# Where 16 weight slots lie in SBUF, modulo 256 bytes

## The chip, the cores and the metric

The kernel runs on one core of a Trainium2 chip. Its time is in device microseconds, from the first to the last instruction with the little around them; runs are compared by their medians. A core has TensorE (PE in the profile, with weight loads apart as PEld), VectorE (DVE), ScalarE (ACT), GpSimd (POOL) and SyncE (SP, which issues the DMAs here). SBUF is the on-chip memory: 128 partitions, and in each a range of byte addresses. A tile takes the same byte range in every partition.

## What is computed

A decoder trunk of 4 layers on 256 tokens of width 1024, in float32. Each layer has three sublayers: a half-step SwiGLU FFN, a token mixer (latent attention, differential attention, Mamba-2, latent attention), and another half-step FFN. So 12 sublayers stand in a row, and each needs the one before it.

```python
cond = silu(c)
for i in range(4):
    mod = (cond @ w_mod[i] + b_mod[i]).reshape(-1, 3, 3, 1024)   # shift, scale, gate
    for j, f in enumerate((ffn(i, 0), mixer(i), ffn(i, 1))):
        h = x * (1 + scale_j) + shift_j
        x = layernorm(8 ** 0.25 * x + weight_j * gate_j * f(h), ln_g[i, j], ln_b[i, j])

def ffn(h):                                  # w_in (1024, 5632), w_out (2816, 1024)
    gate, up = split(h @ w_in)
    return (silu(gate) * up) @ w_out
```

All weights are read once from HBM, about 500 MB in float32 together with `w_mod`.

## The kernel before

**Precision and the three matmuls.** Every product with a weight matrix is made of two fp32r parts of each operand, a high and a low one. For each block of 128x128 weights `mm3` issues three matmuls into one PSUM bank: high weights with high rows, high weights with low rows, low weights with high rows. The weights are the stationary operand. The rows that stream past them are 256 tokens wide (258 in the first products of a sublayer, which carry two more columns).

**Tiles.** `Slots` makes a row of tiles of one kind in SBUF, one behind the other, and hands them out. `wraw` (8 slots of 4096 bytes a partition) receives raw weights from DMA. `wr` (16 slots of 4096 bytes) holds the split weights: ScalarE writes the high part into one slot, VectorE the low part into another. A half-item is one `wraw` slot, thus two `wr` slots, which are nearly always a pair, slots 2p and 2p+1. `hwh` and `hwl` hold the high and low part of the rows that enter a sublayer; `g` has 25 slots that hold, among other things, the high and low rows for the second product of an FFN or a mixer. In most of the kernel a half-item has four 128-row blocks of two 128-column blocks, so 4 x 2 x 3 = 24 matmuls.

**Addresses.** Tiles stand in SBUF in the order in which they are made: `g`, `wraw`, `gacc`, `res`, `t256`, `sd`, `re`, `hwh`, `hwl`, then `wr`, then small tiles and constants. Every tile ahead of `wr` is a multiple of 256 bytes long, so they all begin at the same place modulo 256, and so does the first `wr` slot. `WSTEP = 16` (L422) puts 16 float32, 64 bytes, behind every second slot:

```python
for i in range(n):
    self.tiles.append(self.make(i, dt))
    if step and i % 2:
        pool.tile([128, step], F32, name=f"{name}gap{i}", tag=f"{name}gap{i}")
```

Counted from the streaming rows modulo 256, the eight pairs thus begin at 0, 64, 128, 192, 0, 64, 128, 192. Within a slot a 128x128 block begins at a multiple of 512 bytes, and so does a 256-column row in `hwh`, `hwl` and `g`. Rows of the 258-column products lie 1152 bytes apart.

**Order.** `Program` records all operations, gives each a slot (the one that has been free longest) and an engine, and plans their times with a table of costs; then it issues them in the order of the planned starts. Neither slots nor costs know an address. All instructions stand on the line of that loop, L400.

**Background.** Between the weights, `w_mod` streams through `wraw`, and VectorE sums it up into `gacc` for the shifts, scales and gates of later sublayers.

Of the kernel before, what the change touches and what calls it, by code (L numbers as in the profile page):

```python
# [10 lines left out]
F32 = mybir.dt.float32  # L11
F32R = mybir.dt.float32r
# [43 lines left out]
class Ref:  # L56


    def __init__(self, root, fns):
        self.root, self.fns, self.ap = root, fns, None  # L60
# [52 lines left out]
class Slots:  # L113

    def __init__(self, pool, name, n, elems, psum=False, dt=F32, fresh=False, step=0):
        self.pool, self.name, self.elems, self.psum, self.dt, self.fresh = pool, name, elems, psum, dt, fresh
        self.tiles = []
        for i in range(n):  # L120
            self.tiles.append(self.make(i, dt))
            if step and i % 2:
                pool.tile([128, step], F32, name=f"{name}gap{i}", tag=f"{name}gap{i}")
        self.free = list(range(n))
        self.hist, self.old, self.owner = [[] for _ in range(n)], [[] for _ in range(n)], [None] * n

# [292 lines left out]

WHOLE = (4, 7, 10)  # L420

WSTEP = 16  # L422

DEFER = {0: 3, 1: 3}

# [2 lines left out]
def trunk(ctx: ExitStack, tc: tile.TileContext, consts, x, c, positions, w_mod, b_mod, ln_g, ln_b,  # L428
# [8 lines left out]
    sb = ctx.enter_context(tc.tile_pool(name="sb", bufs=1))  # L437
    pp = ctx.enter_context(tc.tile_pool(name="pp", bufs=1, space=PSUM))
    PW, HP = S + 2, 288
    slots = {}  # L440

    def pool(name, n, elems, dt=F32, step=0):
        slots[name] = Slots(sb, name, n, elems, dt=dt, fresh=name == "g", step=step)

    slots["mm"] = slots["aux"] = Slots(pp, "mm", 8, 512, True)
    for name, n, elems in (("g", 25, 512), ("wraw", 8, 1024), ("gacc", 1, 3072), ("res", 1, 2048),
                           ("t256", 14, 256), ("sd", 1, 512), ("re", 1, 512)):
        pool(name, n, elems)
    for name, n, elems in (("hwh", 1, KD * HP), ("hwl", 1, KD * HP)):
        pool(name, n, elems, F32R)  # L450
    pool("wr", 16, 1024, F32R, WSTEP)
    for name, n, elems in (("dtr", 1, 128), ("w0", 1, 32), ("modc", 6, 24)):
        pool(name, n, elems)

# [308 lines left out]
    class Tail:  # L763
        def __init__(self, s, res, weight):
            self.s, self.d = s, res
            self.weight, self.w = weight, None
# [878 lines left out]
```

## Time and profile before

| | |
|---|---|
| median of 3 runs | 2103.96 us (2102.66 to 2103.96) |
| the profiled execution's own time | 2103.96 us |
| its span, first to last instruction | 2102.2 us |
| TensorE busy | 2074.9 us, 99% |
| VectorE busy | 1713.0 us, 81% |
| ScalarE busy | 1190.2 us, 57% |
| DMA, mean over the span | 240 GB/s |
[...]

How to read it: matmuls are pipelined. [...] How fast the matmuls go through is seen from the distance of their starts (timeline) or from their number in a stretch (table by stretch). The timeline merges neighbours of one kind into one row; in the FFN's first product `hwl` comes once among three matmuls, so it has rows of its own.

### The profile page before, as it was taken

How to read it: one execution, taken by the hardware profiler on the slowest of the kernel's cores; microseconds unless marked ns; L12 is line 12 of the kernel's file. 1: busy time of each engine (PE TensorE's matmuls, PEld its weight loads, DVE VectorE, ACT ScalarE, POOL GpSimd, SP SyncE). 2: the span in 40 equal slices, each digit the busy share in tenths (PEclk: the TensorE clock that was granted, in tenths of full speed). 3: DMA queues.
4: the chain of work that ended last, by engine and by line, in shares of the span. 5: the costliest groups of instructions: out<-in, count | busy, mean ns of one | idle time of the engine just before them, and what ended most of it. 6: DMA issues, size and time to landing. Idle time of an engine off the chain costs nothing. (4 is left out here: it accounts for less than half of the span.)

```text
span 2102.2 us, 42927 instructions
## 1 busy us (share of the span) xinstructions
PE 2074.9 (99%) x17287; PEld 2011.6 (96%) x17287; DVE 1713.0 (81%) x2745; ACT 1190.2 (57%) x1836; POOL 98.5 (5%) x112
## 2 busy tenths in 40 slices
PE   8999999999999999999999999999999999999998
PEld 6999999999999999999999988899999999999998
DVE  4888899887887879977988798879887988879744
ACT  3554687536544786644654475547545644577543
POOL 0000100000000101000000011000000000100000
PEclk9999999999999999999999999999999999999999
DMA  9899657995989435997698654356986889545861
GB/s 312 281 346 326 206 188 249 342 304 187 319 309 324 149 103 161 350 326 256 191 354 304 206 159 140 112 157 197 355 281 205 302 305 323 163 130 186 261 186 45
DMA packets 410227, 504.58 MB, mean 240 GB/s; under 512 B 21937, under 2 KB 371244, under 8 KB 410028
## 3 DMA queue, kind: packets, MB, share of 16 engines
q1 hardware_dynamic: 410028, 501.84, 72.5%
q8 instruction: 135, 2.21, 0.4%
q14 instruction: 64, 0.52, 0.1%
HBM read 500.73 MB, written 1.05 MB: 239 GB/s over the span
## 5 line engine op out<-in xcount | busy, mean ns | idle before, releaser
L400 PE MATMUL mm<-hwh,wr 128*128 128x256 f32 (+1 forms) x6736 | 1222.2, 283 | 3.7 <-ACT hwh L400 1.9
L400 PEld LDWEIGHTS mm<-hwh,wr 128*128 128x128 f32 x6736 | 1041.1, 189 | 19.9 <-issue 14.1
L400 ACT ACTIVATE wr<-wraw 128x1024 fp32r<-128x1024 f32 (+3 forms) x705 | 700.7, 1003 | 577.2 <-PE mm L400 242.9
L400 PE MATMUL mm<-hwl,wr 128*128 128x256 f32 (+1 forms) x3368 | 955.7, 284 | 4.9 <-DVE hwl L400 4.8
L400 DVE TENSOR_TENSOR wr<-wraw,wr 128x1024 fp32r<-128x1024 f32 (+3 forms) x691 | 793.7, 1165 | 172.4 <-ACT wr L400 169.1
L400 PE MATMUL mm<-g,wr 128*128 128x256 f32 x5496 | 665.2, 282 | 1.4 <-DVE g L400 0.9
L400 PEld LDWEIGHTS mm<-g,wr 128*128 128x128 f32 x5496 | 652.9, 189 | 12.3 <-issue 8.3
L400 PEld LDWEIGHTS mm<-hwl,wr 128*128 128x128 f32 x3368 | 637.4, 189 | 11.1 <-DVE hwl L400 6.8
L400 DVE SCALAR_TENSOR_TENSOR gacc<-wraw,condc,gacc 128x1024 f32<-128x1024 f32 x238 | 307.2, 1291 | 7.9 <-DMA wraw<-in_w_mod_dram 7.2
L400 ACT ACTIVATE g<-mm 128x512 f32<-128x512 f32 (+4 forms) x208 | 105.7, 521 | 100.3 <-PE mm L400 98.7
L400 ACT ACTIVATE g<-g 128x512 fp32r<-128x512 f32 (+1 forms) x104 | 63.3, 625 | 36.0 <-DVE g L400 35.6
L400 PE MATMUL mm<-g,g 128*128 128x128 f32 (+2 forms) x464 | 81.6, 312 | 0.0
L400 DVE TENSOR_TENSOR g<-g,g 128x512 fp32r<-128x512 f32 (+2 forms) x111 | 75.4, 699 | 4.2 <-ACT g L400 3.4
L400 DVE TENSOR_TENSOR res<-res,re 128x256 f32<-128x256 f32 x171 | 68.0, 418 | 8.2 <-ACT re L400 7.9
L400 DVE TENSOR_TENSOR g<-g,mm 128x512 f32<-128x512 f32 x81 | 54.9, 680 | 19.6 <-PE mm L400 16.9
L400 PEld LDWEIGHTS mm<-g,g 128*128 128x128 f32 (+1 forms) x464 | 57.9, 175 | 7.4 <-ACT g L400 0.5
L400 ACT ACTIVATE t<-res 128x256 f32<-128x256 f32 x84 | 34.8, 416 | 48.1 <-DVE res L400 47.9
L400 POOL TENSOR_TENSOR res<-res,t 128x256 f32<-128x256 f32 x28 | 25.4, 932 | 708.9 <-ACT t L400 624.9
L400 DVE TENSOR_TENSOR res<-res,t 128x256 f32<-128x256 f32 x56 | 31.7, 581 | 23.9 <-ACT t L400 23.9
L400 DVE SCALAR_TENSOR_TENSOR res<-mm,gw,res 128x256 f32<-128x256 f32 x84 | 39.2, 475 | 14.2 <-PE mm L400 14.2
L400 ACT ACTIVATE t<-res,abcol 128x256 f32<-128x256 f32 x72 | 43.2, 601 | 9.3 <-DVE res L400 8.0
L400 ACT ACTIVATE res<-res,abcol 128x256 f32<-128x256 f32 x88 | 48.0, 588 | 0.0
(198 smaller groups left out, 1158.5 us busy)
## 6 DMA issues: line engine op xcount, KB each, us to landing
wraw<-in_ffn_w_in_dram SPq DMA_DIRECT2D x340, 512.0 KB, 6.1
wraw<-in_w_mod_dram SPq DMA_DIRECT2D x272, 512.0 KB, 6.8
wraw<-in_ffn_w_out_dram SPq DMA_DIRECT2D x128, 512.0 KB, 5.7
wraw<-in_ffn_w_out_dram SPq DMA_DIRECT2D x64, 384.0 KB, 5.7
wraw<-in_ssm_w_in_dram SPq DMA_DIRECT2D x32, 512.0 KB, 4.3
wraw<-in_diff_w_in_dram SPq DMA_DIRECT2D x24, 512.0 KB, 4.3
wraw<-in_w_mod_dram SPq DMA_DIRECT2D x32, 256.0 KB, 6.2
wraw<-in_mla_w_out_dram SPq DMA_DIRECT2D x16, 512.0 KB, 4.6
```

Source lines behind the costliest of these rows:

```text
L400: getattr(eng.real, method)(*[real(a) for a in args], **{k: real(v) for k, v in one.items()})
```

## The change

The gap behind every second slot becomes a list of gaps ahead of slots, `WGAPS`. The first pair has 16 float32 (64 bytes) ahead of it, each later pair 32 (128 bytes). Counted from the streaming rows modulo 256, the pairs now begin at 64, 192, 64, 192, 64, 192, 64, 192. All gaps together grow from 512 to 960 bytes, so everything that is made after `wr` (constants and small tiles) moves up by 448 bytes.

```diff
-    def __init__(self, pool, name, n, elems, psum=False, dt=F32, fresh=False, step=0):
+    def __init__(self, pool, name, n, elems, psum=False, dt=F32, fresh=False, gaps=()):
         self.tiles = []
         for i in range(n):
+            if gaps and gaps[i]:
+                pool.tile([128, gaps[i]], F32, name=f"{name}gap{i}", tag=f"{name}gap{i}")
             self.tiles.append(self.make(i, dt))
-            if step and i % 2:
-                pool.tile([128, step], F32, name=f"{name}gap{i}", tag=f"{name}gap{i}")
...
-WSTEP = 16
+WGAPS = [16, 0] + [32, 0] * 7
...
-    pool("wr", 16, 1024, F32R, WSTEP)
+    pool("wr", 16, 1024, F32R, WGAPS)
```

The instructions do not move. TensorE, before the change, in the first product of an FFN, where it goes over from pair 7 (`wr14`, `wr15`) to pair 1 (`wr2`, `wr3`); `mm` are PSUM banks, and the last number of a name counts the tiles in the order in which they were made:

```order
L400 MATMUL mm1_62<-hwh0_120,wr15_144 128x256
L400 MATMUL mm1_62<-hwh0_120,wr14_143 128x256
L400 MATMUL mm1_62<-hwl0_121,wr14_143 128x256
L400 MATMUL mm1_62<-hwh0_120,wr15_144 128x256
L400 MATMUL mm7_68<-hwh0_120,wr2_125 128x256
L400 MATMUL mm7_68<-hwl0_121,wr2_125 128x256
L400 MATMUL mm7_68<-hwh0_120,wr3_126 128x256
```

The same place of TensorE's order after the change:

```order
L400 MATMUL mm1_62<-hwh0_120,wr15_145 128x256
L400 MATMUL mm1_62<-hwh0_120,wr14_144 128x256
L400 MATMUL mm1_62<-hwl0_121,wr14_144 128x256
L400 MATMUL mm1_62<-hwh0_120,wr15_145 128x256
L400 MATMUL mm7_68<-hwh0_120,wr2_126 128x256
L400 MATMUL mm7_68<-hwl0_121,wr2_126 128x256
L400 MATMUL mm7_68<-hwh0_120,wr3_127 128x256
```

Slots, banks and order are the same; only the count in the slots' names is one higher, since a gap now stands ahead of the first slot. The other four engines' orders are equal in the same sense.

## Rows read from the trace of the kernel before

**Rows 1.** The page: span and busy shares of the engines.

```profile
span 2102.2 us, 42927 instructions
PE 2074.9 (99%) x17287; PEld 2011.6 (96%) x17287; DVE 1713.0 (81%) x2745; ACT 1190.2 (57%) x1836; POOL 98.5 (5%) x112
```

**Rows 2.** Groups by shape: xcount | busy us, mean ns | idle before, releasers.

```profile
L400 PE MATMUL mm<-hwh,wr 128*128 128x256 f32 x5984 | 1082.5, 283 | 3.7 <-ACT hwh L400 1.9 <-ACT g L400 1.0 <-DVE wr L400 0.5
...
L400 PE MATMUL mm<-hwl,wr 128*128 128x256 f32 x2992 | 847.3, 283 | 1.8 <-DVE hwl L400 1.8
...
L400 PE MATMUL mm<-g,wr 128*128 128x256 f32 x5496 | 665.2, 282 | 1.4 <-DVE g L400 0.9 <-ACT g L400 0.2
...
L400 PE MATMUL mm<-hwh,wr 128*128 128x258 f32 x752 | 141.0, 285 | 0.0
```

**Rows 3.** By stretch: us, PE, PEld, DVE, ACT, POOL busy, clock, DMA share, GB/s.

```profile
850.00:1000.00 150.00, 150.00 (x1269) 148.44 (x1268) 121.26 (x142) 72.86 (x90) 1.86 (x2) 1.00 0.90 308
1050.00:1200.00 150.00, 150.00 (x1293) 147.84 (x1292) 124.36 (x158) 75.96 (x98) 5.53 (x5) 1.00 0.90 302
1450.00:1600.00 150.00, 150.00 (x1274) 148.49 (x1273) 122.21 (x134) 73.06 (x88) 0.00 (x0) 1.00 0.94 321
```

**Rows 4.** Timeline of TensorE, FFN at 1453 us: start us, length us, operation.

```profile
1453.79 0.28 PE L400 MATMUL mm<-hwl,wr 128*128 128x256 f32 x1
...
1456.62 0.28 PE L400 MATMUL mm<-hwl,wr 128*128 128x256 f32 x1
...
1459.45 0.28 PE L400 MATMUL mm<-hwl,wr 128*128 128x256 f32 x1
...
1462.32 0.27 PE L400 MATMUL mm<-hwl,wr 128*128 128x256 f32 x1
...
1465.16 0.28 PE L400 MATMUL mm<-hwl,wr 128*128 128x256 f32 x1
...
1467.98 0.28 PE L400 MATMUL mm<-hwl,wr 128*128 128x256 f32 x1
...
1470.36 0.28 PE L400 MATMUL mm<-hwl,wr 128*128 128x256 f32 x1
```

**Rows 5.** Timeline of TensorE, FFN at 358 us, pair 7 then pair 1.

```profile
358.62 0.28 PE L400 MATMUL mm<-hwl,wr 128*128 128x256 f32 x1
...
361.34 0.28 PE L400 MATMUL mm<-hwl,wr 128*128 128x256 f32 x1
...
363.72 0.28 PE L400 MATMUL mm<-hwl,wr 128*128 128x256 f32 x1
```

**Rows 6.** Timeline of TensorE, Mamba-2 mixer at 1256 us, pair 7 then pair 1.

```profile
1256.35 0.44 PE L400 MATMUL mm<-g,g 128*64 128x128 f32 x4
...
1257.30 0.28 PE L400 MATMUL mm<-hwl,wr 128*128 128x256 f32 x1
...
1258.72 0.28 PE L400 MATMUL mm<-hwl,wr 128*128 128x256 f32 x1
...
1261.19 0.28 PE L400 MATMUL mm<-hwl,wr 128*128 128x256 f32 x1
```

**Rows 7.** By stretch of 50 us, columns as in rows 3.

```profile
300.00:350.00 50.00, 48.40 (x408) 47.19 (x407) 48.09 (x99) 37.35 (x64) 3.30 (x4) 1.00 0.67 212
350.00:400.00 50.00, 50.00 (x430) 50.00 (x430) 47.52 (x51) 29.68 (x35) 1.33 (x1) 1.00 1.02 359
...
1100.00:1150.00 50.00, 50.00 (x435) 48.85 (x434) 44.29 (x52) 22.11 (x26) 0.56 (x1) 1.00 0.89 306
```

**Rows 8.** Groups by shape: transposes that stream the identity.

```profile
L400 PE MATMUL mm<-cst,g 128*128 128x128 f32 x140 | 28.6, 277 | 1.8 <-DMA g<-in_x_dram 1.0 <-ACT g L400 0.6 <-DVE g L400 0.2
```

More of the change, by code (lines that the diff above doesn't have):

```diff
@@ L440, in trunk, with pool @@
     slots = {}
-    def pool(name, n, elems, dt=F32, step=0):
-        slots[name] = Slots(sb, name, n, elems, dt=dt, fresh=name == "g", step=step)
+    def pool(name, n, elems, dt=F32, gaps=()):
+        slots[name] = Slots(sb, name, n, elems, dt=dt, fresh=name == "g", gaps=gaps)
     slots["mm"] = slots["aux"] = Slots(pp, "mm", 8, 512, True)
```

## Prediction, made before the changed kernel ran

> **What bounds the kernel now.** I read the page's busy shares first. TensorE is busy 2074.9 of 2102.2 us; VectorE, next, has 1713.0 [rows 1]. So the end is set by how fast TensorE gets through its matmuls. The chain that ended last names only the output's tail and says nothing on this. The groups by shape come next: 5,984 + 2,992 + 5,496 = 14,472 matmuls stream 256 columns past a 128x128 block of weights from a `wr` slot [rows 2]. Their "mean 283 ns" is a pipelined length, not a price. The price is the step from one start to the next, and two views give it.
>
> The table by stretch gives the mean. Three FFN stretches of 150 us, each with TensorE busy 150.00, hold 1269, 1293 and 1274 matmuls [rows 3]: 450,000 ns / 3,836 = 117.3 ns a step. A few short matmuls are among them, so 117.3 may be low by some tenths.
>
> The timeline gives the steps one slot pair at a time. In [rows 4] I kept, of six successive half-items, the second matmul (the one with `hwl`), and of the last half-item also the final one. The half-items are 24 matmuls each, and by the program's order they use the pairs 5, 3, 0, 6, 7, 1 (pair p is slots 2p and 2p+1). What a reader should call the distance is (slot's address minus address of the streaming row) modulo 256. Streams lie in `g`, `hwh` and `hwl`, all at the same place modulo 256, and the rows and blocks in them are multiples of 512 bytes, so before the change pair p has distance 64p modulo 256. Start to start, over 24:
>
> - pair 5, distance 64: 2.83 us, 117.9 ns
> - pair 3, distance 192: 2.83 us, 117.9 ns
> - pair 0, distance 0: 2.87 us, 119.6 ns
> - pair 6, distance 128: 2.84 us, 118.3 ns
> - pair 7, distance 192: 2.82 us, 117.5 ns
> - pair 1, distance 64: 1467.98 to 1470.36, 21 steps, 113.3 ns
>
> Same shapes, same streams, no idle time named in any row: the placement is what differs, though not alone. At 64 and 192 there are two paces, 113.3 and about 117.8. In [rows 5] pair 7 at distance 192 takes 2.72 us over 24 (113.3) and pair 1 behind it, at 64, 2.38 us over 21 (113.3). At 0 and 128 no run that I followed was quick.
>
> So the quick pace has a memory. It survives a change from 192 to 64 [rows 5]. A slow run at 192 can turn quick at the change to 64, as the last two half-items of [rows 4] do. And it need not: after `g,g` matmuls came in between, pair 7 went on at 118.3 (1257.30 to 1258.72, 12 steps) and pair 1 stayed slow, 117.6 over 21 steps [rows 6].
>
> **The change part by part.** No instruction is added, removed or moved: the order of every engine is the same, as the rows of the program's order show. Three things happen.
>
> *The slots move.* After it even pairs lie at distance 64 and odd ones at 192; none at 0 or 128. Every one of the 14,472 steps is then quick (113.3) or slow (117.8). Let f be the share of quick ones: the mean step is 117.8 - 4.5 f. Bounds of f: if no run ever turns quick, 0; if all do, 1. What I take: some 12,000 of the 14,472 are in the eight FFNs (by the loops 44 x 8 and 8 x 22 blocks, 3 matmuls each: 1,584 an FFN, less 96 of 258 columns in seven of them), where TensorE never idles in [rows 3]; once quick, a run there stays quick until something interrupts it, and every change from 192 to 64 is another chance to become so. I take 0.92 there and 0.5 in the mixers, which interrupt often: (12,000 x 0.92 + 2,472 x 0.5) / 14,472 = 0.85. The step is then 114.0, the saving 14,472 x (117.3 - 114.0) = 47.8 us. With f = 0.95: 113.5, 55 us; with f = 0.45: 115.8, 21.7 us.
>
> The 1,128 matmuls of 258 columns (752 in [rows 2], and half as many with `hwl`) stream from rows 1,152 bytes apart, so their distance jumps by 128 from row to row. After the change they too meet 64 and 192 only. I take nothing for them; at the same 3.3 ns it would be 3.7 us more, at the same amount the other way 3.7 less.
>
> *The feed has to keep up.* Splits on ScalarE and VectorE and the weight DMAs must deliver 3% sooner. VectorE has 48.09 us of work in 300 to 350, DMA a share of 1.02 in 350 to 400 [rows 7]. Against a shortage: the stretch at 1050 held 1293 matmuls and the one at 850 only 1269, at DMA share 0.90 both and VectorE 124.36 and 121.26, and TensorE idled in neither [rows 3]. A pace 1.9% higher has been fed already without a wait. Bounds: nothing, or all the gain of the 17 fifty-microsecond windows in which VectorE has 44 us or more (the highest and lowest of them in [rows 7]): 850 / 2102.2 x 47.8 = 19.3 us. I take 4, near nothing, by [rows 3].
>
> *What lies behind the slots moves by 448 bytes*, 192 modulo 256: the constants, with the identity that transposes stream. Its distance from the `g` tiles goes from 64 to 128. The 140 transposes in [rows 8] and some 230 like them, at 119.6 - 113.3 = 6.3 ns at worst, are 2.3 us. Below nothing I see no reason, since 128 is the dearer place. I take nothing: most stand alone, not back to back.
>
> [...]
>
> Sum: 2103.96 (the profiled execution's own time, 1.8 us over its span, and the median of the runs) - 47.8 + 4 = 2060.
>
> **The rivals.**
>
> *The pace is drawn anew and kept.* If only interruptions decide it, f is about what 64 and 192 have now. The mean step 117.3, with half at 0 and 128 (119.6 and 118.3, mean 119.0), leaves 115.6 for the other half, f = 0.49; and 14,472 x 1.7 = 24.6 us. Less 4 of waits: 2083. For it [rows 6]; against it the last two half-items of [rows 4].
>
> *VectorE becomes the bound* in the 17 windows: the gain is 47.8 - 19.3 = 28.5, the time 2075.
>
> *The slow pace locks in: slower.* In [rows 4] pairs 5 and 3 pass the slow pace on, 64 to 192, with no loss of it. Perhaps it is the passage through 0 or 128 that shifts the weights' reading against the stream's and lets a later pair be quick; pairs 0 and 6 stand between the slow pairs and the quick one. The change takes these passages away. Then f = 0, every step is 117.8, and the time 2103.96 + 14,472 x 0.5 = 2111. It decides below f = (117.8 - 117.3) / 4.5 = 0.11. Against it: the last quick run is entered from 192 directly, and quick is kept through 192 to 64.
>
> *It does nothing.* The steps may follow something that only goes along with the slot, such as the bank written or the item; then 2104. That pairs 5 and 1, both at 64, differ speaks a little for it. [...]
>
> **How the numbers follow.** Forecast 0.68, alone 2046 to 2072: the low end is f = 0.95 with no waits (2103.96 - 55 = 2049), less 3 for the 258-column steps, the high end f = 0.65 (113.3 + 0.35 x 4.5 = 114.9, 34.7 us) with 4 of waits, 2073. Pace drawn anew 0.12, 2072 to 2092. VectorE bound 0.10, 2066 to 2084. Locked slow 0.04. Nothing 0.05, the rule on ports 0.03 of it. Another 0.01. From 2046 to 2086 holds nearly all of the first and third and over half of the second, about 0.83. A measurement can tell about 0.2% (4.2 us) from no change. Faster by more: 0.90; within: 0.05; slower: 0.05.
>
> **What would show it.** FFN stretches of 150 us that hold 1,300 to 1,325 matmuls where they held 1,269 to 1,293; runs of 24 at 2.72 us (113.3) through pairs of both distances in the timeline; no 119.6 anywhere in the FFNs. If the rival of the kept pace is right, whole FFNs run at 117.8 and others at 113.3, with the border at an interruption. If VectorE binds, TensorE's row shows idle time "<-DVE wr" or "<-ACT wr" around 300 and 850. If the slow pace locks, 1,272 in every stretch. The prediction is wrong if the steps change but the span does not follow, or if a half-item at 64 or 192 shows 119.6.

## The result and the profile after

The changed kernel takes 2057.45 us (median of four runs, 2054.45 to 2059.70) against 2103.96: a ratio of 0.978, 95% interval 0.9761 to 0.9799. One more run of before took 5206.11 us; it is left out of the ratio, and nothing else of it is on record. The change takes 46.5 us off, where the prediction took 43.96 off and gave 2060. The profiled execution took 2054.45 us, 1.75 over its span.

The page's span and busy shares, the lines that answer to [rows 1]:

```profile
span 2052.7 us, 42927 instructions
...
PE 2024.5 (99%) x17287; PEld 1961.1 (96%) x17287; DVE 1714.4 (84%) x2745; ACT 1194.5 (58%) x1836; POOL 98.5 (5%) x112
```

The counts are those of before. TensorE's busy time fell by 50.4 us and the span by 49.5; VectorE's busy time did not move. So the time came out of the matmuls themselves, not out of idle time. The groups by shape, as in [rows 2]:

```profile
L400 PE MATMUL mm<-hwh,wr 128*128 128x256 f32 x5984 | 1052.2, 279 | 3.5 <-ACT hwh L400 1.9 <-ACT g L400 1.0 <-DVE wr L400 0.4
...
L400 PE MATMUL mm<-hwl,wr 128*128 128x256 f32 x2992 | 837.3, 280 | 1.8 <-DVE hwl L400 1.8
...
L400 PE MATMUL mm<-g,wr 128*128 128x256 f32 x5496 | 645.5, 278 | 1.5 <-DVE g L400 0.9 <-ACT g L400 0.3
```

The idle time before the groups is as it was. The mean of one fell by about 4 ns of a length of 280 that still says little; the table by stretch says it plainly (columns as in [rows 3]; the third and the fourth of these stretches are two of the three there, and the stretch at 1050 now reaches into a mixer):

```profile
350.00:500.00 150.00, 150.00 (x1321) 147.91 (x1321) 127.42 (x160) 80.03 (x102) 6.39 (x5) 1.00 0.89 305
550.00:700.00 150.00, 150.00 (x1314) 147.86 (x1314) 128.36 (x182) 81.03 (x108) 8.12 (x20) 1.00 0.84 287
850.00:1000.00 150.00, 150.00 (x1319) 147.91 (x1318) 125.77 (x172) 78.65 (x105) 2.74 (x3) 1.00 0.86 290
1450.00:1600.00 150.00, 150.00 (x1317) 147.91 (x1316) 126.60 (x177) 78.78 (x105) 2.74 (x3) 1.00 0.84 282
```

The stretch at 850 held 1269 matmuls and holds 1319; the one at 1450 held 1274 and holds 1317. TensorE is busy throughout these stretches in both kernels. And the timeline (start us, length us, operation), first `hwl` matmul of seven successive half-items, in the order of pairs 2, 3, 4, 5, 6, 0, 7, which after the change lie at 64, 192, 64, 192, 64, 64, 192:

```profile
356.51 0.28 PE L400 MATMUL mm<-hwl,wr 128*128 128x256 f32 x1
...
359.23 0.28 PE L400 MATMUL mm<-hwl,wr 128*128 128x256 f32 x1
...
361.95 0.28 PE L400 MATMUL mm<-hwl,wr 128*128 128x256 f32 x1
...
364.67 0.28 PE L400 MATMUL mm<-hwl,wr 128*128 128x256 f32 x1
...
367.39 0.28 PE L400 MATMUL mm<-hwl,wr 128*128 128x256 f32 x1
...
370.11 0.28 PE L400 MATMUL mm<-hwl,wr 128*128 128x256 f32 x1
...
372.83 0.28 PE L400 MATMUL mm<-hwl,wr 128*128 128x256 f32 x1
```

Six times 2.72 us for 24 matmuls, 113.3 ns a step, through pairs of both distances. In [rows 4] such a row of half-items took 2.83, 2.83, 2.87, 2.84, 2.82.

**Steps of the whole program.** For this and all later runs I took every two neighbouring `wr` matmuls of 256 columns in the trace, start to start, where the step is below 160 ns (no wait and no other matmul between), and gave each its slot by the program's order. These are about 14,010 of the 14,472. "Quick" is a step below 116 ns. At 64 and 192 these are the steps of the quick pace; at 128 they are single short steps between longer ones (0.05 of the 0.26 of before). The span then falls into three parts:

| | steps of 256 columns | mean ns | quick | steps of 258 columns, us | rest of the span, us | span, us |
|---|---|---|---|---|---|---|
| before | 14,014: 1647.2 us | 117.54 | 0.26 | 127.3 | 327.7 | 2102.2 |
| after | 14,009: 1596.2 us | 113.94 | 0.87 | 126.7 | 329.7 | 2052.7 |

The steps of 256 columns gave 51.0 us, those of 258 columns 0.6, and the rest took 2.0 back: 49.5 (rounded parts) in this execution.

### The profile page after: what moved, and what is told of

The parts are those of the page before. It is cut to its first block, busy times and chain, and to the rows that moved or that the text cites. A ratio compares the mean times of both kernels' runs of the same rounds, so it can differ in the third digit from the quotient of the medians.

```text
span 2052.7 us, 42927 instructions
## 1 busy us (share of the span) xinstructions
PE 2024.5 (99%) x17287; PEld 1961.1 (96%) x17287; DVE 1714.4 (84%) x2745; ACT 1194.5 (58%) x1836; POOL 98.5 (5%) x112
## 5 line engine op out<-in xcount | busy, mean ns | idle before, releaser
L400 PE MATMUL mm<-hwh,wr 128*128 128x256 f32 (+1 forms) x6736 | 1191.3, 280 | 3.5 <-ACT hwh L400 1.9
L400 PEld LDWEIGHTS mm<-hwh,wr 128*128 128x128 f32 x6736 | 1028.4, 189 | 19.7 <-issue 14.0
L400 PE MATMUL mm<-hwl,wr 128*128 128x256 f32 (+1 forms) x3368 | 945.5, 281 | 5.6 <-DVE hwl L400 5.5
L400 PE MATMUL mm<-g,wr 128*128 128x256 f32 x5496 | 645.5, 278 | 1.5 <-DVE g L400 0.9
L400 PEld LDWEIGHTS mm<-g,wr 128*128 128x128 f32 x5496 | 633.4, 188 | 12.4 <-issue 7.4
L400 ACT ACTIVATE t<-res 128x256 f32<-128x256 f32 x84 | 34.8, 417 | 46.7 <-DVE res L400 46.5
```

The source lines that it names most:

```text
L400: getattr(eng.real, method)(*[real(a) for a in args], **{k: real(v) for k, v in one.items()})
```

## The experiments

**Theory**: the weights' distance from the stream, modulo 256 bytes, sets which paces a step can have (0 and 128: slow only; 64 and 192: 113.3 or 117.8), and the pace is kept until something interrupts; turns from 192 to 64 are further chances to become quick. **Rivals**: being off 0 and 128 is all that matters and the turns do nothing; the place of the constants, or of everything, does it and not the slots' distance. Each edit below is against the changed kernel, and every kernel of this section has the instructions and the order of before; only addresses differ. `WGAPS` counts floats of 4 bytes ahead of each slot.

**All pairs at one distance.** All at 64:

```
-WGAPS = [16, 0] + [32, 0] * 7
+WGAPS = [16] + [0] * 15
```

> All 16 slots at distance 64 from the streaming rows, no turns. Theory (a run that goes on slow after an interruption turns quick only where the distance goes from 192 to 64): without turns each stretch keeps the pace it starts with, about half quick, mean step 115.4 ns, 2057 + 14,472 x 1.5 ns = 2079 us. Rival (64 and 192 are alike, and only 0 and 128 cost): 2057 as the change.

Measured: 2075.14 us (2068.51 to 2077.95), ratio to before 0.9854 (0.9831 to 0.9877). Its steps are 115.34 ns in the mean, 0.55 quick. Three stretches (columns as in [rows 3]):

```profile
350.00:400.00 50.00, 50.00 (x427) 50.00 (x426) 47.23 (x51) 29.61 (x35) 1.59 (x1) 1.00 1.04 364
...
550.00:600.00 50.00, 50.00 (x444) 50.00 (x443) 46.56 (x48) 28.29 (x34) 0.00 (x0) 1.00 1.02 358
...
1950.00:2000.00 50.00, 50.00 (x427) 50.00 (x426) 28.02 (x28) 21.95 (x26) 0.00 (x0) 1.00 0.60 198
```

All three are FFN without an idle moment, one at about 113 ns and two at about 117. Without turns a pace lasts until something comes in between, and that happens inside an FFN too. In the one from which the first stretch comes, the steps are slow up to 409.5 and quick from 411.6 to 485.2, and between the two stand eight small matmuls:

```profile
409.61 0.28 PE L400 MATMUL mm<-hwl,wr 128*128 128x256 f32 x1
409.82 0.64 PE L400 MATMUL mm<-gacc,ones 128*32 128x256 f32 x8
410.39 0.51 PE L400 MATMUL mm<-hwh,wr 128*128 128x256 f32 x2
```

By means over nine steps, no change of pace in this trace comes without an interruption ahead of it. In the stretch 1950 to 2000 the change itself is quick (444 matmuls). The feed is not what differs: the slow stretch at 1950 has the least DMA share and VectorE work of the three. So 64 alone gives 1.46 of the 2.2 per cent, and two distances by turns the other third; the rival that turns do nothing expected the change's own time and falls.

All at 192:

```
-WGAPS = [16, 0] + [32, 0] * 7
+WGAPS = [48] + [0] * 15
```

> All 16 slots at distance 192, no turns. Theory: after an interruption runs at 192 start slow (31 of 32 that I followed in the changed kernel's trace) and nothing turns them, so nearly all steps are 117.8 ns: 2057 + 14,472 x 3.7 ns = 2110 us, slower than before. Rival (64 and 192 alike, only 0 and 128 cost): 2057.

Measured: 2098.15 us (2095.36 to 2100.29), ratio 0.9966 (0.9955 to 0.9978); 116.91 ns, 0.20 quick. Slow nearly all through, but not as much as expected: 2110, slower than before, was expected, and it is 0.3% quicker than before. A few stretches are quick, one of them here:

```profile
550.00:600.00 50.00, 50.00 (x427) 50.00 (x426) 44.71 (x45) 26.15 (x30) 0.00 (x0) 1.00 0.98 342
900.00:950.00 50.00, 50.00 (x442) 49.45 (x441) 40.91 (x46) 23.32 (x27) 0.00 (x0) 1.00 0.83 289
```

An interruption can leave a run at 192 quick too, more seldom than at 64 (0.20 of all steps are quick, 0.55 with all slots at 64). That step of the theory ("192 nearly always starts slow") was too strong.

All at 0, and all at 128:

```
+WGAPS = [0] * 16          (all at 0)
+WGAPS = [32] + [0] * 15   (all at 128)
```

> All 16 slots at distance 0, no gaps at all. If the distance sets the step, nearly every 256-column step is 119.9 ns: 2104 + 14,472 x 2.4 ns = 2139 us. Rival (the steps follow something that only goes along with the slot, such as the item or the bank): about 2104.

> All 16 slots at distance 128. By the steps at 128 in the kernel before, about 118.5 ns whatever came ahead, and no quick pace at all: 2057 + 14,472 x 4.6 ns = 2123 us. Rival (128 is dear only in the change from and to other distances, and has a quick pace of its own when nothing turns): below 2104.

Measured: 2135.64 us at 0 and 2122.08 at 128, one execution each; 119.93 and 118.84 ns. At 0 hardly a step is below 116 ns; at 128 0.17 of them are, most of 115 ns, but never two in a row. Neither has a quick run. The stretch 350 to 400, first at 0, then (second fence) at 128:

```profile
350.00:400.00 50.00, 50.00 (x419) 50.00 (x418) 46.30 (x49) 28.92 (x35) 1.35 (x1) 1.00 1.01 354
```

```profile
350.00:400.00 50.00, 50.00 (x424) 50.00 (x423) 47.01 (x50) 28.81 (x35) 1.40 (x1) 1.00 1.01 355
```

From 419 to 424 to 443 matmuls in 50 us (0, 128, the change), for the same instructions. Both times came within 4 us of what was expected. The rival that the steps follow the item or the bank and not the slot is gone with these two: only the addresses of the slots and of what lies behind them changed, and the spans are longer than that of before and of the change. A placement that cannot matter would give one time for all these kernels; measured are 2135.6 to 2055.0. Where in the chip the time is lost is not shown, since a trace has no single reads. One thing the runs do not separate: the streaming rows and the other tiles ahead of `wr`, the raw weights among them, begin at one place modulo 256, so every edit moves the slots against all of these at once. That the step goes with the slot that TensorE is reading speaks for the streaming rows.

**The constants alone.** The slots as before, and the constants behind them moved by 448 bytes, as the change moves them:

```
-WGAPS = [16, 0] + [32, 0] * 7
+WGAPS = [0, 0] + [16, 0] * 7
+    (a tile of 128 floats behind the last slot: the 16 of before and 112 more)
```

> The slots as before the change (distances 0, 64, 128, 192), and only what lies behind them moved up by 448 bytes, as the change does. Theory (the gain is the slots', the constants' place costs 0 to 2.3 us): 2104 to 2106 us. Rival (part of the gain comes from the constants' new place): below 2100.

Measured: 2105.13 us (2103.13 to 2108.08), ratio 1.0004 (0.9994 to 1.0013); 117.56 ns, 0.26 quick, as before. The constants' place is worth nothing that ten executions show.

**Everything moved together.** The change, with 64 bytes more ahead of all tiles, so that streams and weights both move and the distance stays:

```
+    sb.tile([128, 16], F32, name="ahead", tag="ahead")
```

> The changed kernel with 64 bytes more ahead of all tiles, so that streams, slots and constants all move by 64 and every distance stays. Theory (the distance counts, not the place): 2057 us, within the spread of its runs of 2054 to 2060. Rival (the place of the slots modulo 256 counts: they now lie where slots at distance 0 and 128 lay before): 2104 plus 14,472 x 1.7 ns = 2128 us.

Measured: 2057.14 us (2054.70 to 2059.03), ratio 0.9773 (0.9757 to 0.9789); 113.92 ns, 0.87 quick. Two stretches of it:

```profile
350.00:400.00 50.00, 50.00 (x444) 50.00 (x443) 47.45 (x51) 31.64 (x38) 1.40 (x1) 1.00 1.05 368
...
1950.00:2000.00 50.00, 50.00 (x443) 50.00 (x442) 27.29 (x27) 22.83 (x26) 0.00 (x0) 1.00 0.58 185
```

It is the distance that counts, and not the address.

**Places in between.** Pairs at 32 and 160, and pairs at 96 and 224:

```
+WGAPS = [8, 0] + [32, 0] * 7    (32 and 160)
+WGAPS = [24, 0] + [32, 0] * 7   (96 and 224)
```

> The changed kernel's turns at distances 32 and 160 instead of 64 and 192. If only the 64-byte step in which the distance lies counts, these read as 0 and 128, and the mean step is 119.2 ns: 2057 + 14,472 x 5.3 ns = 2134 us. If the pace changes evenly with the distance, half way: about 116.6 ns, 2096 us. If any distance off 0 and 128 will do: 2057.

> Turns at distances 96 and 224. If only the 64-byte step in which the distance lies counts, these read as 64 and 192: 2057 us. If the pace changes evenly with the distance, about 116.6 ns a step, 2096 us. If any distance off 0 and 128 will do: 2057 too.

Measured: 2124.57 us and 2099.92 us, one execution each. The first has 118.3 ns at 32 and 119.8 at 160, the second 117.8 at 96 and 116.7 at 224, and in neither is the quick pace kept over a half-item: never more than three steps below 116 ns stand in a row. The stretch 350 to 400 of each:

```profile
350.00:400.00 50.00, 50.00 (x422) 50.00 (x421) 46.89 (x50) 29.59 (x36) 1.29 (x1) 1.00 1.02 357
```

```profile
350.00:400.00 50.00, 50.00 (x429) 50.00 (x429) 47.49 (x51) 29.10 (x36) 2.34 (x1) 1.00 1.04 363
```

None of the readings written down fits both: an even change with the distance (2096) comes near the second and misses the first. "Any place off 0 and 128 will do" wanted 2057 and falls; neither pair of distances behaves as 64 and 192 do, and the two differ by 25 us from each other. What holds is only that of the eight distances tried, 64 and 192 alone can keep 113.3.

**Turning more often.** Neighbouring slots, and so the high and the low part of one block, at 64 and 192 by turns:

```
-WGAPS = [16, 0] + [32, 0] * 7
+WGAPS = [16] + [32] * 15
```

> Slots alternate singly: even ones at distance 64, odd ones at 192, so the distance turns two times within every three matmuls instead of once in a half-item. Theory (192 to 64 turns slow into quick): the slow stretches after interruptions end after a few matmuls, all steps near 113.4 ns: 2057 - 14,472 x 0.5 ns = 2050 us, and less spread between runs. Rival (the pace is drawn at an interruption and kept, turns or not): 2057. Against both: if the high and the low part of the weights have to lie at one distance, the step is a new one, up to 118 ns and 2115 us.

Measured: 2056.60 us (2053.66 to 2057.46), ratio 0.977 (0.9755 to 0.9784); 113.95 ns, 0.89 quick. No gain on the change, though turns are now between single matmuls. The timeline at the start of an FFN says why (pairs 6, 0, 7, 1, whose high parts lie at 192 here, then from 333.31 pair 2, whose high part lies at 64):

```profile
324.16 0.28 PE L400 MATMUL mm<-hwl,wr 128*128 128x256 f32 x1
...
333.08 0.28 PE L400 MATMUL mm<-hwl,wr 128*128 128x256 f32 x1
...
334.14 0.28 PE L400 MATMUL mm<-hwl,wr 128*128 128x256 f32 x1
...
341.62 0.28 PE L400 MATMUL mm<-hwl,wr 128*128 128x256 f32 x1
```

From 324.16 to 333.08 are 75 steps of 118.9 ns, from 334.14 to 341.62 66 of 113.3. Through some 50 turns the slow pace stayed, at a little more than 117.8, and it went quick within 0.7 us of the first high part at 64. So a turn from 192 to 64 does not of itself end the slow pace; the expected gain fails on this. By sublayer, its Mamba-2 mixer is quicker than the change's (114.8 against 115.8 ns a step), the other three mixers are slower (116.1 against 114.8), and the FFNs are alike (113.68 and 113.70).

**Six pairs at 64, two at 192.** If the run at 64 is the one that can become quick after an interruption, and the turn the other chance, fewer places at 192 should do no harm:

```
-WGAPS = [16, 0] + [32, 0] * 7
+WGAPS = [16, 0] + [0, 0] * 2 + [32, 0] * 2 + [0, 0] * 2 + [32, 0]
```

> Three pairs at distance 64 to one at 192. Theory (a run starts quick about every second time at 64 and hardly ever at 192; the turn from 192 to 64 ends a slow one, and quick is kept through turns): more quick starts but fewer turns, so about the change's time, 2055 to 2065 us. Rival (the draw alone decides and is kept): with three quarters at 64, f about 0.45, mean step 115.8 ns, 2084 us.

Measured: 2054.97 us (2052.21 to 2056.92), ratio 0.9761 (0.9748 to 0.9774); 113.86 ns, 0.89 quick. It is the lowest median here, 3.4 us below the change on the same chip (next paragraph). All five executions there lie below all four of the change (2057.26 to 2059.53), but the intervals of the two ratios overlap, and the steps account for only 1.2 us (113.86 against 113.94 ns): the best of the kernels tried, and whether it gains on the change is not settled. Two places at 192 of eight are enough.

**The change again**, on the chip of that run, to learn what makes its executions differ by 5 us:

> The changed kernel once more, beside the one before it on the same chip: 2057 us, 2054 to 2060. If its spread comes from the pace that is drawn at interruptions, the share of quick steps in this profile differs from the first one's 0.87 by some hundredths, and the time with it by 14,472 x 4.5 ns = 0.65 us for each hundredth.

Measured: 2058.32 us (2057.26 to 2059.53) against 2105.1 of before there, ratio 0.9777 (0.9764 to 0.979). The time came as expected, but the reason offered for the spread did not show: the steps are the same in the execution of 2054.45 us and in this one of 2057.26 (113.94 ns and 0.87 quick both, 1596.2 and 1597.2 us). The rest of the span differs, 329.7 against 334.0, mostly because some 20 steps of 258 columns between 311 and 318 take about 214 ns here and so are counted in it. The stretches from 305 to 320 show why, first of the change's first profile, then of this one (columns as in [rows 3], the clock third from last):

```profile
305.00:310.00 5.00, 3.61 (x32) 3.41 (x31) 4.97 (x13) 3.95 (x7) 0.00 (x0) 1.00 0.26 84
310.00:315.00 5.00, 4.62 (x38) 4.62 (x39) 5.00 (x13) 3.29 (x9) 0.00 (x0) 1.00 0.12 33
315.00:320.00 5.00, 5.00 (x45) 5.00 (x44) 3.96 (x11) 2.79 (x4) 0.96 (x1) 1.00 0.76 216
```

```profile
305.00:310.00 5.00, 3.66 (x33) 3.46 (x31) 4.97 (x13) 3.95 (x7) 0.00 (x0) 1.00 0.21 69
310.00:315.00 5.00, 4.49 (x24) 4.49 (x24) 3.72 (x9) 3.41 (x9) 0.00 (x0) 0.63 0.13 43
315.00:320.00 5.00, 5.00 (x32) 5.00 (x32) 4.34 (x11) 0.36 (x1) 0.95 (x1) 0.69 0.64 206
```

TensorE stands still for 1.8 us (1.39 and 0.38 in the first two rows) and for 1.9 us (1.34 and 0.51). Then the granted clock stays at 1.00 in one and falls in the other, to means of 0.63 and 0.69 in the last two rows: at half of full speed, as in the fall of the first profile (0.50 from 1184.2 to 1190.8), that is 2 x (0.37 + 0.31) x 5 = 6.8 us, an estimate. The two rows have 27 matmuls fewer. Each profile has a fall at the very end, from about 2048. Besides that the first has one too, in the mixer at 1184, again of 6.8 us (granted clock 0.93 in the stretch 1150 to 1200); this one has a second there of half that length, at 1188 (0.97). The 3.4 us more at half clock are worth about 1.7 of the 2.8 us between the two executions, an estimate; the steps of 256 columns add 1.0. The profile of before has one short fall, near 1214 (0.97 in 1200 to 1250), and none around 310, though TensorE stood still for 1.6 us of the stretch from 315 to 320 there; nor is there one behind a pause of 1.9 us at 311 in the kernel with everything moved (granted clock 0.998 over its span). Why the clock falls in one execution and not in another after the same pause stays open.

## Why the prediction was right, and where its steps were off

**Paces and placement.** Right. 113.3 and 117.8 at 64 and 192, about 119.6 at 0 and 118.3 at 128 [rows 4, 5] hold over whole programs: 119.93 and 118.84 with every slot at 0 and at 128, and stretches of 113.3 and of 117.8 with every slot at 64. In the trace of before, pairs of one distance modulo 256 have one mean step (119.8 and 119.7 at pairs 0 and 4, 118.5 and 118.4 at pairs 2 and 6), which bears out the count modulo 256. Reading the steps of single pairs from the timeline was enough to come within 2.6 us of the median.

**The share of quick steps and the sum.** The prediction took f = 0.85 and a mean of 114.0 ns; measured are 0.87 and 113.94. It took 117.3 for before, where all steps together give 117.54 (it said that 117.3 may be low). Its saving of 47.8 compares with 51.0 in the profile. The split was good too: the steps of all FFNs have 0.92 quick (taken: 0.92; 113.70 ns), and the four FFN stretches above, 5,271 matmuls in 600 us, give 113.8 ns. In the mixers the share was taken as 0.5 and is 0.58 over all, by mixer 0.82, 0.64, 0.47 and 0.66. Both shares were choices and not worked out from rows: that turns would bring the share up was argued, that it came out so near was partly luck. The lowest share is that of the Mamba-2 mixer, 0.26 between 1250 and 1300. The timeline of the change there (the transposes in front, then pair 6 at 64) shows a slow start:

```profile
1256.64 0.93 PE L400 MATMUL mm<-cst,g 128*128 128x128 f32 x7
1257.33 0.36 PE L400 MATMUL mm<-hwh,wr 128*128 128x256 f32 x1
1257.53 0.28 PE L400 MATMUL mm<-hwl,wr 128*128 128x256 f32 x1
...
1260.36 0.28 PE L400 MATMUL mm<-hwl,wr 128*128 128x256 f32 x1
```

After other matmuls and a short wait, 24 steps at 64 take 2.83 us, 117.9. This is the case of [rows 6], and it goes on after the change.

**The memory of the pace.** In the change's trace, turns with at least five steps on either side behave so: quick from 192 into 64, quick after it in 202 of 202; quick from 64 into 192, 222 of 222; slow from 192 into 64, quick after it in 25 of 30; slow from 64 into 192, still slow in 15 of 17. After an interruption, runs at 192 begin slow in 31 of 32 and at 64 quick in 23 of 43 (at 64 mostly after one to four longer steps, of 116 to 124 ns). So "survives a turn" and "a turn is another chance" were right for this kernel, and the run with all slots at 64 shows that the second of them is worth some 17 us (2075.14 against 2057.45 and 2058.32). As a general rule the second is wrong: with turns between single matmuls the slow pace lasted through dozens of them.

**The feed.** The prediction took 4 us of new waits. TensorE's waits (engine, line, waited for: us, times, longest us) for the operands that ScalarE and VectorE make, after:

```profile
PE mm L400 <- DVE hwl L400: 5.5, 8, 1.8
...
PE mm L400 <- ACT g L400: 2.4, 6, 1.0
...
PE mm L400 <- ACT hwh L400: 1.9, 2, 1.4
...
PE mm L400 <- DVE wr L400: 0.4, 1, 0.4
```

and before:

```profile
PE mm L400 <- DVE hwl L400: 4.8, 7, 1.6
...
PE mm L400 <- ACT hwh L400: 1.9, 2, 1.4
PE mm L400 <- ACT g L400: 1.8, 4, 1.0
...
PE mm L400 <- DVE wr L400: 0.5, 1, 0.5
```

The first three are 1.3 us more together, not 4, and none of it is a wait for split weights (`wr`), the shortage that the prediction had in mind: that one is 0.4 after and 0.5 before. The rest of the span grew by 2.0 in all; the fall of the clock at 1184, 6.8 us where before has 3.4, would cover what is left, but that was not tested. The argument from a stretch that had already been fed faster [rows 3] was the right one, and the 4 us were too careful. The stretch 350 to 400 of the change, against its row in [rows 7], and the one ahead of it:

```profile
300.00:350.00 50.00, 48.23 (x419) 48.03 (x419) 48.01 (x94) 35.81 (x58) 1.37 (x2) 1.00 0.67 211
350.00:400.00 50.00, 50.00 (x443) 50.00 (x443) 47.82 (x51) 31.68 (x38) 1.36 (x1) 1.00 1.06 371
```

443 matmuls where there were 430, with VectorE at 47.82 and the DMA share at 1.06, and TensorE without idle time: this window, one of those that the rival "VectorE becomes the bound" had named, took the new pace.

**Steps of 258 columns and constants.** Both were taken as nothing: 0.6 us and, by the run with the constants alone, 1.0004 of before.

**The rivals.** The pace kept as drawn (2083) is near what happens without turns: 2075.14 with all slots at 64, 2098.15 at 192. The slow pace locked in by turns (2111) does not occur in this change, and occurs in stretches where every matmul turns; the passages through 0 and 128 are not needed to become quick. That nothing happens is refuted by the change and by the placements above, 2054.97 to 2135.64 us with the same instructions. For the rule on ports, on which 0.03 of that chance was put, no run shows anything: the mean steps, 113.86 to 119.93 ns by placement alone, show only that the distance counts.

**The remainder.** The saving was taken 3.2 us too low (47.8 for 51.0), the steps of 258 columns 0.6 too low, and the new waits 2.0 too high (4 for 2.0): all the same way, so that 2060 stands 5.6 above the profiled execution's 2054.45. The median stands only 2.55 below the forecast because that execution was the fastest of its four. The term that was off most is the mean step of before: 117.3 from three FFN stretches with some short matmuls among them, 117.54 by the steps, 0.24 ns or 3.5 us over 14,472 of them. The step after was off by 0.06 ns only, 0.9 us.

## What to carry to other kernels

Where matmuls follow each other back to back and TensorE is never idle, measure the step from start to start for each weight buffer on its own: here, with 256 columns, buffers of equal work differed by their addresses alone (in the kernel before, 118.4 to 118.5 ns in the mean at pairs 2 and 6 and 119.7 to 119.8 at pairs 0 and 4). In this kernel, weight slots at 64 modulo 128 bytes from the moving rows, some at 64 and some at 192 modulo 256, took 3.7% off the slowest placement tried (2135.6 to 2057.5 us) without one instruction changed. Such a pace was kept for long (with all slots at 64 it stayed slow from 1886.4 to 2026.7 us without a break), so a placement should be judged by whole stages and several executions, not by one half-item.

## What the runs showed of the hardware beyond that

The lowest pace at which steps of 256 columns with a weight block of their own went on was 113.3 ns, in every kernel that was quick anywhere; the other mean steps were 117.8 (slow at 64 and 192), 118.8 (128) and 119.9 (0), and 116.7 to 119.8 at 32, 96, 160 and 224. The two paces at one and the same distance, with all slots at 64 the quick one kept over some 650 steps (411.6 to 485.2 us) and the slow one over some 1,190 (1886.4 to 2026.7), were the least expected. What decides after an interruption which of them begins, and why 64 begins quick more often than 192, is not settled by these runs; nor is what in the chip makes the distance count, nor why the places 32 bytes off give neither pace.
